# Hybrid attention block on one core: probabilities times values as two fp32r passes over four heads at once

## The chip, the cores and the metric

The kernel runs on one core of one Trainium2 chip, as one launch. The metric is the device time of an execution in microseconds (us), the median of repeated runs. TensorE is called PE (its weight loads PEld), VectorE DVE, ScalarE ACT, GpSimd POOL, SyncE SP. "fp32r" is the type in which PE takes a 32-bit operand in one pass at reduced precision; a full-precision operand is carried as a pair of fp32r tiles, "high" (the rounded value) and "low" (what the rounding left).

## What is computed

A transformer block on 512 tokens of width 1024: a mixer with three attention branches (a: stick-breaking, b: attention over the keys that an index score selects, c: a gated sum of compressed, selected-block and windowed attention), then attention over a memory of 256 tokens, then a gated feed-forward layer. Only branches b and c matter here. For each of them, cut to the core:

```python
s = jnp.einsum('bqhd,bkd->bhqk', qb, k) * scale      # four heads share one key head
p = _masked_softmax(s, mask)
o = jnp.einsum('bhqk,bkd->bqhd', p.astype(v.dtype), v)   # four heads share one value head, 64 wide
# branch c: gb[...,0:1]*o_cmp + gb[...,1:2]*o_sel + gb[...,2:3]*o_win
```

With 512 tokens, every selected block and the window cover all earlier keys, so `o_sel` and `o_win` are causal attention over two different key and value sets; branch b takes the 128 best keys of each query by its score. `o_cmp` runs over at most 31 compressed keys.

## The kernel before, in words

The kernel is written for a scheduler that takes the program order as priority: it lays out each engine's queue when the program is built, moving an instruction ahead of others that are not ready. So matrix products of later parts fill PE while the attention chains wait on other engines. Buffers come from pools; a tile name in a pool is a ring of `bufs` buffers.

Weights come through two rings. `load_split` (line 88) takes a raw buffer (name "raw", three of them in the pool `stage`), lets SP load 512 KB into it, copies the high part on ACT (line 58) and subtracts the low part on DVE (line 66) into one of three buffer pairs ("whi", "wlo"). `load_fill` (line 89) is the same with two buffers of each kind in the pool `fill`, and its subtraction runs on POOL. A product of two split operands is `mm3` (lines 91 to 96): high by high, high by low, low by high, all fp32r.

The part around the change, in program order: the projections (lines 524 to 552); the loop of branch c over four row tiles of 128 queries (lines 619 to 624); the gates of branch a (`fill_gate(0, f)`, line 627) and its up-projection (`merge_up(0, ...)`, 628); the gates of branch c (630); the 16 rounds that pick the top 128 scores, on DVE (631 to 633); the up-projection of branch c (634, weights through `load_split`); the masks from the scores (638); the loop of branch b over four row tiles (640 to 643); the gates of branch b (646), eight products named f = 0 to 7 over half the tokens, of which the odd ones take their weights through `load_split` and the even ones through `load_fill` (line 378); then the memory's norm, keys and values (663 to 683, weights through `load_split`).

A row tile of attention is `rows_attention` (570 to 590): per head two products give the scores (line 292, 293), DVE adds the mask and finds the negated maximum (578), ACT takes the exponential and its sum (579); then the rows are scaled (586 on ACT in branch c, 588 on DVE in branch b), and `apply_v` (561 to 568) runs once for each 128 keys: four transposes on PE into one PSUM bank (565), one copy to SBUF (568 calls line 58 on ACT for branch c, line 60 on DVE for branch b), and `pair` (98 to 101): two full fp32 products of the 64-wide value with two heads' probabilities each (256 columns), one into PSUM partitions 0 to 63 and one into 64 to 127. `cmp_attention` (592 to 610) does the same for the compressed keys with 32-row transposes. A row tile ends with `split(..., scale=0.5)` from PSUM into o_hi (68, ACT) and o_lo (69, DVE).

The constants (identity, masks, rotary tables) are one tile `cst`, loaded in two pieces (191, 305).

Of the kernel before, what the change touches and what calls it, by code (L numbers as in the profile page):

```python
# [26 lines left out]
def block_kernel(ctx: ExitStack, tc: tile.TileContext, A, out, dbg=None):  # L27
# [13 lines left out]
    fill_st = ctx.enter_context(ExitStack())  # L41
    fill = pool(fill_st, "fill", side="right")
    utp = pool(ctx, "ut")
    cst = const.tile([P, 1408], F32, name="cst")
    nc.scalar.preload_act_table_set("natural_log_exp_and_others")
    ident = cst[:, 0:128]
    causal = cst[:, 384:896]
    cmpb = cst[:, 896:1024].rearrange("p (h n) -> p h n", n=32)
    rope_t = cst[:, 1024:1536 - 128].rearrange("p (t c d) -> p t c d", t=3, d=32)
    eps = const.tile([P, 1], F32, name="eps")  # L50
    nc.vector.memset(eps, 1e-6)
    one = const.tile([P, 1], F32, name="one")
# [93 lines left out]
    def cc(c):  # L146
        return slice(c * P, (c + 1) * P)
# [154 lines left out]
    for c in range(NT):  # L302
        for i, post in enumerate((post_qa, post_ka, post_va)):
            project_chunk(c, 256, w_a[8 * i:8 * i + 8], post)
    nc.sync.dma_start(cst[:, 128:], A["cst"][:, 128:])
    nc.vector.memset(fixed[:, 3, :].bitcast(F32), -1.0)
    nc.vector.tensor_copy(fixed[:, 0:3, :], cst[:, 0:384].rearrange("p (a b) -> p a b", b=128))
    flush()
    w0_st.close()

# [115 lines left out]
    kwin = k_pair(bc, "kwin")  # L426
    vs = {n: bc.tile([P, NT, 64], F32, name=n) for n in ("vb", "vsel", "vwin")}
    kc = k_pair(bc, "kc", 32)
    vc = bc.tile([32, 64], F32, name="vc")
    score = [None] + [bc.tile([P, (i + 1) * P], F32, name=f"score{i}") for i in range(1, NT)]  # L430
    early_st = mix.enter_context(ExitStack())
    early = pool(early_st, "early")
# [5 lines left out]
    cw = pool(cw_st, "cw")  # L438
    pw_st = mix.enter_context(ExitStack())
    pw = pool(pw_st, "pw2")  # L440

    def post_g1(c, p):

# [54 lines left out]
    def compressed(hid):  # L498
        hs = cw.tile([P, 512], F32, name="rel", bufs=2)
        v, t = hs[0:32, 0:256], hs[0:32, 256:512]  # L500
        nc.scalar.copy(v, hid[0:32].rearrange("p a b -> p (a b)"))
        nc.vector.tensor_mul(t, v, v)
        nc.vector.tensor_scalar(t, t, 0.044715, 1.0, op0=ALU.mult, op1=ALU.add)
        nc.vector.tensor_mul(t, t, v)
        nc.scalar.activation(t, t, AF.Exp, scale=-1.5957691216057308)
        nc.vector.tensor_scalar(t, t, 1.0, None, op0=ALU.add)
        nc.vector.reciprocal(t, t)
        nc.vector.tensor_mul(v, v, t)
        tp = ps.tile([P, 512], F32, name="ps")
        for x in range(2):  # L510
            nc.tensor.transpose(tp[:, 32 * x:32 * x + 32], v[:, 128 * x:128 * x + 128], ident[0:32, 0:32])
        ht = cw.tile([P, 2, 32], F32, name="ht")
        nc.vector.tensor_copy(ht, tp[:, 0:64].rearrange("p (a b) -> p a b", b=32))
        w2t = cw.tile([P, 3, 64], F32, name="w2t")
        for i in range(2):
            nc.scalar.dma_start(w2t[:, i, :], A["cmp_w2_k"][0])
        nc.scalar.dma_start(w2t[:, 2, :], A["cmp_w2_v"][0])
        res = ps.tile([P, 512], F32, name="ps")
        nc.tensor.matmul(res[:, 0:32], w2t[:, 0:2, :].rearrange("p a d -> p (a d)"), ht[:, 0, :], start=True, stop=True)
        nc.tensor.matmul(res[0:32, 64:128], ht[:, 1, :], w2t[:, 2, :], start=True, stop=True)  # L520
        split(kc[0], kc[1], res[:, 0:32])
        nc.vector.tensor_copy(vc, res[0:32, 64:128])

    project([(1732, 256)], 4, post_g2)
    project([(1024, 128), (1408, 68), (1988, 140)], 3, post_g1)
# [32 lines left out]
    mq_st = mix.enter_context(ExitStack())  # L558
    mq = pool(mq_st, "mq")

    def apply_v(o_ps, v, src, first, last, k=P, eng=nc.scalar):

        tp = ps.tile([P, 4, P], F32, name="ps")
        for h in range(4):
            nc.tensor.transpose(tp[0:k, h, :], src[:, h, :], ident)
        pt = mq.tile([P, 4, P], F32, name="pt", bufs=3)
        copy(eng, pt[0:k], tp[0:k])
        pair(o_ps, [v, v], [pt[0:k, x::2, :] for x in range(2)], first, last)

    def rows_attention(i, q, k, v, bias, gate, o_ps, first, last, eng=nc.scalar):  # L570
        n = (i + 1) * P
        pr = mq.tile([P, 4, 512], F32, name="pr", bufs=2)
        nm = mq.tile([P, 4], F32, name="nm", bufs=2)
        den = mq.tile([P, 4], F32, name="den", bufs=2)
        for h in range(4):
            st = gm_ps.tile([P, 512], F32, name="gm")
            scores(st[:, :n], q[:, h, cc(i)], [t[:, 0:n] for t in k])
            nc.vector.tensor_tensor_reduce(pr[:, h, :n], st[:, :n], bias, -1.0, 3e38, ALU.add, ALU.min, nm[:, h:h + 1])
            nc.scalar.activation(pr[:, h, :n], pr[:, h, :n], AF.Exp, bias=nm[:, h:h + 1], scale=-1.0, accum_out=den[:, h:h + 1])
        sc = mq.tile([P, 4], F32, name="sc", bufs=2)  # L580
        nc.vector.reciprocal(sc, den)
        if gate is not None:
            nc.vector.tensor_mul(sc, sc, gate)
        for h in range(4):
            if eng is nc.scalar:
                nc.scalar.activation(pr[:, h, :n], pr[:, h, :n], AF.Copy, scale=sc[:, h:h + 1])
            else:
                nc.vector.tensor_scalar(pr[:, h, :n], pr[:, h, :n], sc[:, h:h + 1], None, op0=ALU.mult)
        for j in range(i + 1):
            apply_v(o_ps, v[:, j, :], pr[:, :, cc(j)], first and j == 0, last and j == i, eng=eng)  # L590

    def cmp_attention(i, o_ps, first, last):
        s = mq.tile([P, 4, 32], F32, name="cs")
        st = ps.tile([P, 4, P], F32, name="ps")
        for h in range(4):
            scores(st[:, h, 0:32], qc[:, h, cc(i)], kc)
        nc.vector.tensor_add(s, st[:, :, 0:32], cmpb[:, i, :].unsqueeze(1).to_broadcast([P, 4, 32]))
        m = mq.tile([P, 4], F32, name="nm", bufs=2)
        nc.vector.tensor_reduce(m, s, axis=AX.X, op=ALU.max)
        nc.vector.tensor_scalar(m, m, -1e20, None, op0=ALU.max)  # L600
        nc.vector.tensor_sub(s, s, m.unsqueeze(2).to_broadcast([P, 4, 32]))
        nc.scalar.activation(s, s, AF.Exp)
        den = mq.tile([P, 4], F32, name="den", bufs=2)
        nc.vector.tensor_reduce(den, s, axis=AX.X, op=ALU.add)
        nc.vector.tensor_scalar(den, den, 1e-30, None, op0=ALU.max)
        sc = mq.tile([P, 4], F32, name="sc", bufs=2)
        nc.vector.reciprocal(sc, den)
        nc.vector.tensor_mul(sc, sc, gates[:, i, 0::3])
        nc.vector.tensor_mul(s, s, sc.unsqueeze(2).to_broadcast([P, 4, 32]))
        apply_v(o_ps, vc, s, first, last, k=32)  # L610

    def topk_rounds(i, n):
        for _ in range(n):
            m8 = mq.tile([P, 8], F32, name="m8", bufs=3)
            nc.vector.max(m8, score[i])
            nc.vector.match_replace(score[i], m8, score[i], -3e38)

    o_c = o_pair("c", mq)
    for i in range(NT):
        o_ps = av_ps.tile([P, 2, P], F32, name="av")  # L620
        cmp_attention(i, o_ps, True, False)
        rows_attention(i, qc, ksel, vs["vsel"], causal_bias(i), gates[:, i, 1::3], o_ps, False, False)
        rows_attention(i, qc, kwin, vs["vwin"], causal_bias(i), gates[:, i, 2::3], o_ps, False, True)
        split(o_c[0][:, :, cc(i)], o_c[1][:, :, cc(i)], o_ps, scale=0.5)
    dump("o_c", o_c[0].bitcast(F32))
    for f in range(early_g, NK):
        fill_gate(0, f)
# [9 lines left out]
    for i in range(1, NT):  # L637
        nc.vector.tensor_scalar(score[i], score[i], -2e38, NEG, op0=ALU.is_gt, op1=ALU.mult)
    o_b = o_pair("b", op)
    for i in range(NT):  # L640
        o_ps = av_ps.tile([P, 2, P], F32, name="av")
        rows_attention(i, qb, kb, vs["vb"], score[i] if i else causal_bias(0), None, o_ps, True, True, nc.vector)
        split(o_b[0][:, :, cc(i)], o_b[1][:, :, cc(i)], o_ps, scale=0.5)
    dump("o_b", o_b[0].bitcast(F32))
    for f in range(NK):
        fill_gate(1, f, S // 2)
# [234 lines left out]
def constants():  # L881
    import numpy as np

    c = np.zeros((128, 1408), np.float32)
    i = np.arange(128)
    c[:, 0:128] = np.eye(128, dtype=np.float32)
    c[:, 128:256] = np.where(i[:, None] >= i[None, :], -1.0, 0.0)
    c[:, 256:384] = np.where(i[:, None] >= i[None, :], NEG, 0.0)
    c[:, 768:896] = np.where(i[None, :] > i[:, None], NEG, 0.0)
    n = np.arange(32)  # L890
    for t in range(4):
        q = t * 128 + i
        c[:, 896 + 32 * t:928 + 32 * t] = np.where((16 * n[None, :] + 31 <= q[:, None]) & (n[None, :] < 31), 0.0, NEG)
    inv = np.float32(10000.0) ** (-np.arange(0, 64, 2, dtype=np.float32) / np.float32(64))
    ang = np.arange(512, dtype=np.float32)[:, None] * inv[None, :].astype(np.float32)
    cos, sin = np.cos(ang), np.sin(ang)
    for t, tab in enumerate((cos, -sin, sin)):
        c[:, 1024 + 128 * t:1152 + 128 * t] = tab.reshape(4, 128, 32).transpose(1, 0, 2).reshape(128, 128)
    return c
# [26 lines left out]
```

## Time and profile before

| | us |
|---|---|
| median of 3 runs (lowest, highest) | 902.41 (901.3, 902.61) |
| the profiled execution's own time | 901.59 |
| its span, first to last instruction | 899.8 |
| PE busy in the span | 859.8 (96%) |
| DVE, ACT, POOL busy | 509.5, 412.3, 139.0 |
| mean granted TensorE clock | 0.990 |

Times in rows are from the span's start. A busy share of PE counts the pipeline of each matmul, so overlapping matmuls are counted once; how fast PE works is read from the distance between matmuls, not from the busy share. In the chain view each piece is the time that one step adds to the chain that ended last. "x4" is a count of instructions; one fp32 product is recorded as two instructions.

### The profile page before, as it was taken

What the parts mean: (1) busy time and instruction counts of PE and PEld (TensorE: products, weight loads), DVE (VectorE), ACT (ScalarE), POOL (GpSimd) and SP (SyncE); (2) the same over time, 40 slices, a digit from 0 to 9 for tenths busy, and PEclk for the clock granted to TensorE, in tenths of its full rate; (3) what the DMA queues carried; (4) which work ended last, traced back from release to release, by engine and by line L of the source; (5) the groups of instructions that cost most, each with busy time, mean ns of one, the idle gap of its engine ahead of it and who ended that gap; (6) DMA issues with size and microseconds to landing.
All of it is one profiled execution on the core that took longest, in us unless ns stands there. A gap on an engine that the chain in (4) does not pass through costs nothing.

```text
span 899.8 us, 13079 instructions
## 1 busy us (share of the span) xinstructions
PE 859.8 (96%) x5012; PEld 734.3 (82%) x5012; DVE 509.5 (57%) x1155; ACT 412.3 (46%) x779; POOL 139.0 (15%) x116
## 2 busy tenths in 40 slices
PE   5999999899999999899989999999999999999995
PEld 5987899887768877778878979998888888888884
DVE  4456378799992067676677758544434333322226
ACT  6488545567772234554655546432232233211123
POOL 4021232202224462230232020000000000000002
PEclk9999999999999999999999999999999999999998
DMA  9340114511212332558445514553333333332312
GB/s 322 84 110 24 52 49 121 139 48 34 62 48 71 94 94 71 186 173 241 128 148 187 178 48 131 179 160 93 94 95 101 105 98 94 117 94 93 97 45 93
DMA packets 93710, 99.00 MB, mean 110 GB/s; under 512 B 4656, under 2 KB 81616, under 8 KB 93648
## 3 DMA queue, kind: packets, MB, share of 16 engines
q1 hardware_dynamic: 91568, 92.75, 34.1%
q10 hardware_dynamic: 2080, 5.42, 1.8%
q8 instruction: 39, 0.64, 0.3%
q14 instruction: 23, 0.19, 0.1%
HBM read 96.06 MB, written 2.10 MB: 109 GB/s over the span
## 4 chain that ended last, share of the span: by engine, by line
PE 83%; DVE 8%; ACT 3%; DMA 3%; issue 2%; POOL 1%; SPq 0%; ACTq 0%; DVEq 0%; POOLq 0%
PE wo L95 9%; PE wo L96 9%; PE wo L94 9%; PE gf L94 5%; PE gf L96 5%; PE gf L95 5%; PE ff L96 4%; PE ff L94 4%; PE ff L95 4%; PE gm L94 3%; PE gm L95 3%; PE gm L96 3%; PE av L101 2%; PE y L96 2%; PE y L95 2%; PE y L94 2%
## 5 line engine op out<-in xcount | busy, mean ns | idle before, releaser
L58 ACT CAST whi<-raw 128x1024 fp32r<-128x1024 f32 (+1 forms) x167 | 174.9, 1050 | 289.0 <-PE y L96 78.9
L66 DVE TENSOR_TENSOR wlo<-raw,whi 128x1024 fp32r<-128x1024 f32 (+1 forms) x131 | 164.2, 1256 | 206.6 <-ACT whi L58 206.2
L66 POOL TENSOR_TENSOR wlo<-raw,whi 128x1024 fp32r<-128x1024 f32 x36 | 87.2, 2428 | 324.2 <-ACT whi L58 277.2
L95 PE MATMUL wo<-ut_lo,whi 128*128 128x256 f32 (+1 forms) x320 | 105.9, 331 | 0.0
L96 PE MATMUL wo<-ut_hi,wlo 128*128 128x256 f32 (+1 forms) x320 | 105.0, 328 | 0.0
L94 PE MATMUL wo<-ut_hi,whi 128*128 128x256 f32 (+1 forms) x320 | 104.7, 327 | 0.0
L96 PE MATMUL gf<-ut_hi,wlo 128*128 128x512 f32 (+1 forms) x192 | 70.0, 365 | 0.0
L94 PE MATMUL gf<-ut_hi,whi 128*128 128x512 f32 (+1 forms) x192 | 69.8, 364 | 0.0
L95 PE MATMUL gf<-ut_lo,whi 128*128 128x512 f32 (+1 forms) x192 | 69.5, 362 | 0.0
L94 PE MATMUL ff<-ut_hi,whi 128*128 128x512 f32 (+1 forms) x192 | 67.9, 354 | 0.0
L95 PE MATMUL ff<-ut_lo,whi 128*128 128x512 f32 (+1 forms) x192 | 67.9, 354 | 0.0
L96 PE MATMUL ff<-ut_hi,wlo 128*128 128x512 f32 (+1 forms) x192 | 67.9, 354 | 0.0
L95 PEld LDWEIGHTS wo<-ut_lo,whi 128*128 128x128 f32 x320 | 61.4, 192 | 6.3 <-issue 1.0
L94 PEld LDWEIGHTS wo<-ut_hi,whi 128*128 128x128 f32 x320 | 61.2, 191 | 5.7 <-issue 0.7
L96 PEld LDWEIGHTS wo<-ut_hi,wlo 128*128 128x128 f32 x320 | 61.3, 192 | 5.5 <-issue 0.4
L875 POOL TENSOR_TENSOR ut_hi<-ut_hi,ut_lo 128x512 f32<-128x512 f32 x4 | 5.0, 1274 | 367.0 <-ACT ut_hi L874 367.0
L94 PE MATMUL gm<-whi,ut_hi 128*128 128x256 f32 (+1 forms) x160 | 47.6, 298 | 0.0
L95 PE MATMUL gm<-wlo,ut_hi 128*128 128x256 f32 (+1 forms) x160 | 46.7, 292 | 0.0
L96 PE MATMUL gm<-whi,ut_lo 128*128 128x256 f32 (+1 forms) x160 | 46.6, 291 | 0.0
L96 PEld LDWEIGHTS gf<-ut_hi,wlo 128*128 128x128 f32 x192 | 36.2, 189 | 6.6 <-issue 1.9
L94 PEld LDWEIGHTS gf<-ut_hi,whi 128*128 128x128 f32 x192 | 36.2, 189 | 6.3 <-issue 1.5
L95 PEld LDWEIGHTS gf<-ut_lo,whi 128*128 128x128 f32 x192 | 36.3, 189 | 5.5 <-issue 0.8
(329 smaller groups left out, 2034.8 us busy)
## 6 DMA issues: line engine op xcount, KB each, us to landing
raw<-in_w_ffn_in_dram SPq DMA_DIRECT2D x56, 512.0 KB, 3.6
raw<-in_w_in_dram SPq DMA_DIRECT2D x46, 512.0 KB, 3.9
raw<-in_w_ffn_out_dram SPq DMA_DIRECT2D x22, 512.0 KB, 3.6
raw<-in_w_out_dram SPq DMA_DIRECT2D x16, 512.0 KB, 3.6
raw<-in_w_up_dram SPq DMA_DIRECT2D x8, 512.0 KB, 3.8
xt<-in_x_dram SPq DMA_DIRECT2D x4, 512.0 KB, 9.2
raw<-in_w_mem_kv_dram SPq DMA_DIRECT2D x4, 512.0 KB, 3.7
raw<-in_w_mem_q_dram SPq DMA_DIRECT2D x4, 512.0 KB, 3.7
```

Source lines behind the costliest of these rows:

```text
L58: nc.scalar.copy(dst, src)
L66: (lo_eng or nc.vector).tensor_sub(dst_lo, src, dst_hi.bitcast(F32))
L94: nc.tensor.matmul(dst, lh, rh, start=first, stop=False, skip_group_check=True)
L95: nc.tensor.matmul(dst, lh, rl, start=False, stop=False, skip_group_check=True)
L96: return nc.tensor.matmul(dst, ll, rh, start=False, stop=last, skip_group_check=True).ins
L101: nc.tensor.matmul(dst[64 * x:64 * x + 64], lhs[x], rhs[x], start=first, stop=last, skip_group_check=True)
L875: nc.gpsimd.tensor_mul(yo[:, n], yo[:, n], gain[:, n])
```

## The change

`apply_v` makes both operands pairs of fp32r. The value of one key tile is stored as its high and low parts side by side in 128 columns; the probabilities of all four heads (512 columns) are the moving operand, once their high part and once their low part. The result fills a whole PSUM bank: partitions 0 to 63 hold what the high part of the value gives, 64 to 127 what its low part gives. After the last key tile of a row tile, the new function `fold` adds the two halves and puts heads where they stood before; its SBUF tile is a "raw" buffer of the pool `stage`. The compressed branch is padded with zeros to 128 keys and takes its rows from the ring "pr". The constants are re-ordered, and the rotary tables and two triangular masks are loaded into pools of their own.

```diff
-    cst = const.tile([P, 1408], F32, name="cst")
+    cst = const.tile([P, 768], F32, name="cst")
...
-    nc.sync.dma_start(cst[:, 128:], A["cst"][:, 128:])
+    tri = pw.tile([P, 2, 128], F32, name="tri")
+    nc.sync.dma_start(tri, A["cst"][:, 768:1024].rearrange("p (a b) -> p a b", b=128))
+    nc.sync.dma_start(cst[:, 128:], A["cst"][:, 128:768])
...
-    nc.vector.tensor_copy(fixed[:, 0:3, :], cst[:, 0:384].rearrange("p (a b) -> p a b", b=128))
+    nc.vector.tensor_copy(fixed[:, 0, :], ident)
+    nc.vector.tensor_copy(fixed[:, 1:3, :], tri)
...
-    vc = bc.tile([32, 64], F32, name="vc")
+    vc = bc.tile([P, 2, 64], F32R, name="vc")
+    nc.gpsimd.memset(vc.bitcast(F32), 0.0)
...
+    rope_t = pw.tile([P, 3, NT, 32], F32, name="rope_t")
+    nc.sync.dma_start(rope_t, A["cst"][:, 1024:1408].rearrange("p (t c d) -> p t c d", t=3, d=32))
...
-        nc.vector.tensor_copy(vc, res[0:32, 64:128])
+        split(vc[0:32, 0, :], vc[0:32, 1, :], res[0:32, 64:128])
...
-    def apply_v(o_ps, v, src, first, last, k=P, eng=nc.scalar):
+    def apply_v(o_ps, v, src, first, last):
         tp = ps.tile([P, 4, P], F32, name="ps")
         for h in range(4):
-            nc.tensor.transpose(tp[0:k, h, :], src[:, h, :], ident)
-        pt = mq.tile([P, 4, P], F32, name="pt", bufs=3)
-        copy(eng, pt[0:k], tp[0:k])
-        pair(o_ps, [v, v], [pt[0:k, x::2, :] for x in range(2)], first, last)
+            nc.tensor.transpose(tp[:, h, :], src[:, h, :], ident)
+        pt = [mq.tile([P, 4, P], F32R, name=n, bufs=2) for n in ("pt_hi", "pt_lo")]
+        split(pt[0], pt[1], tp)
+        for x in range(2):
+            nc.tensor.matmul(o_ps, v.rearrange("p a d -> p (a d)"), pt[x].rearrange("p h q -> p (h q)"),
+                             start=first and x == 0, stop=last and x == 1, skip_group_check=True)
+
+    def fold(o, i, o_ps):
+        ov = o_ps.rearrange("p (a b q) -> p a b q", a=2, b=2)
+        hi, lo = (t[:, :, cc(i)] for t in o)
+        t = stage.tile([P, WT], F32, name="raw", bufs=3)[:, 0:2 * P].rearrange("p (a q) -> p a q", a=2)
+        top, bot = slice(0, 64), slice(64, 128)
+        nc.scalar.copy(t[top], ov[bot, :, 0, :])
+        nc.scalar.copy(t[bot], ov[top, :, 1, :])
+        nc.vector.tensor_add(t[top], ov[top, :, 0, :], t[top])
+        nc.vector.tensor_add(t[bot], ov[bot, :, 1, :], t[bot])
+        split(hi, lo, t, scale=0.5)
...
-        s = mq.tile([P, 4, 32], F32, name="cs")
+        pr = mq.tile([P, 4, 512], F32, name="pr", bufs=2)
+        s = pr[:, :, 0:32]
+        nc.gpsimd.memset(pr[:, :, 32:128], 0.0)
...
-        apply_v(o_ps, vc, s, first, last, k=32)
+        apply_v(o_ps, vc, pr[:, :, 0:128], first, last)
...
+    def two_parts(v):
+        t = mq.tile([P, NT, 2, 64], F32R, name="v2", bufs=2)
+        split(t[:, :, 0, :], t[:, :, 1, :], v)
+        return t
+
+    vsel, vwin = two_parts(vs["vsel"]), two_parts(vs["vwin"])
...
-        o_ps = av_ps.tile([P, 2, P], F32, name="av")
+        o_ps = av_ps.tile([P, 512], F32, name="av")
...
-        split(o_c[0][:, :, cc(i)], o_c[1][:, :, cc(i)], o_ps, scale=0.5)
+        fold(o_c, i, o_ps)
...
+    vb = two_parts(vs["vb"])
...
-        split(o_b[0][:, :, cc(i)], o_b[1][:, :, cc(i)], o_ps, scale=0.5)
+        fold(o_b, i, o_ps)
```

## Rows read from the trace of the kernel before

**Rows 1.** The page, busy time by engine.
```profile
PE 859.8 (96%) x5012; PEld 734.3 (82%) x5012; DVE 509.5 (57%) x1155; ACT 412.3 (46%) x779; POOL 139.0 (15%) x116
```

**Rows 2.** Busy time by stretch: window, length, engines, PE clock, DMA share, GB/s.
```profile
195.00:329.00 134.00, 133.01 (x689) 101.33 (x688) 83.54 (x283) 71.27 (x159) 44.42 (x21) 1.00 0.25 67
329.00:360.00 31.00, 29.30 (x206) 22.79 (x205) 24.74 (x69) 16.12 (x43) 8.42 (x5) 1.00 0.23 69
372.00:377.00 5.00, 0.73 (x8) 0.52 (x6) 4.89 (x5) 2.06 (x4) 3.32 (x2) 0.99 0.75 258
377.00:381.00 4.00, 4.00 (x15) 3.06 (x16) 2.78 (x4) 2.11 (x6) 0.00 (x0) 0.58 0.45 115
```

**Rows 3.** The chain that ended last, 345 to 400 us: start, length, step.
```profile
358.60 0.58 PE av L101 x4
...
376.99 1.09 PE ps L133 x4
...
390.47 0.23 PE gm L96
```

**Rows 4.** Groups of PE's matmuls by shape, 359.2 to 372 us.
```profile
L94 PE MATMUL gf<-ut_hi,whi 128*128 128x256 f32 x35 | 10.0, 285 | 0.0
```

**Rows 5.** Line 101, its instructions: count, ns min/median/max, first and last start.
```profile
L101 PE MATMUL av<-pt,vb x40: 379/404/430, 336.1 to 358.8; 128*64 128x256 f32 x40
```

**Rows 6.** The chain that ended last, 196 to 270 us.
```profile
204.06 0.58 PE av L101 x4
204.65 0.43 PE gf L95
...
234.48 1.45 PE av L101 x12
```

**Rows 7.** Instructions in order of time, 256 to 264 us: PE's matmuls and weight loads.
```profile
259.30 0.40 PE L96 MATMUL gf<-o_hi,wlo 128*128 128x512 f32 x1
259.30 0.19 PEld L94 LDWEIGHTS gf<-o_hi,whi 128*128 128x128 f32 x1
...
259.53 0.40 PE L94 MATMUL gf<-o_hi,whi 128*128 128x512 f32 x1
```

**Rows 8.** Groups of DVE by shape, 329 to 361 us: busy us, mean ns.
```profile
L60 DVE COPY pt<-ps 128x512 f32<-128x512 f32 x10 | 6.4, 687 | 2.4 <-PE ps L565 2.2
...
L66 DVE TENSOR_TENSOR wlo<-raw,whi 128x1024 fp32r<-128x1024 f32 x2 | 2.6, 1304 | 0.0
...
L69 DVE SCALAR_TENSOR_TENSOR o_lo<-av,o_hi 128x256 fp32r<-128x256 f32 x4 | 1.7, 424 | 2.3 <-ACT o_hi L68 2.3
```

**Rows 9.** The instructions on tile pt: the copy on ACT.
```profile
L58 ACT COPY pt<-ps x24: 560/590/617, 201.0 to 267.2; 128x512 f32<-128x512 f32 x20, 32x512 f32<-32x512 f32 x4
```

**Rows 10.** Groups of ACT by shape, 329 to 361 us.
```profile
L58 ACT CAST whi<-raw 128x1024 fp32r<-128x1024 f32 x4 | 4.2, 1048 | 7.0 <-PE gm L95 5.4 <-PE gf L95 1.2 <-issue 0.4
...
L68 ACT ACTIVATE o_hi<-av 128x256 fp32r<-128x256 f32 x4 | 1.5, 384 | 7.8 <-PE av L101 7.8
```

**Rows 11.** Line 616, the last step of the top-128 rounds.
```profile
L616 DVE MATCH_REPLACE8 score<-m,score x48: 409/550/708, 196.6 to 271.8; 128x256 f32<-128x256 f32 x16, 128x384 f32<-128x384 f32 x16, 128x512 f32<-128x512 f32 x16
```

**Rows 12.** The page, DMA issues: KB each, median us to landing.
```profile
raw<-in_w_in_dram SPq DMA_DIRECT2D x46, 512.0 KB, 3.9
```

**Rows 13.** Instructions of DVE in order of time, 63 to 67.2 us.
```profile
65.43 1.16 DVE L66 TENSOR_TENSOR sbwl<-sbs,sbwh 128x512 fp32r<-128x512 f32 x2 [3.45 <-ACT sbwh L58]
66.69 0.69 DVE L331 SCALAR_TENSOR_TENSOR sbs<-ps,sba 128x512 f32<-128x512 f32 x1
```

**Rows 14.** Instructions of ACT in order of time, 62 to 67 us.
```profile
62.29 0.72 ACT L329 ACTIVATE sba<-sba,one 128x512 f32<-128x512 f32 x1
...
66.34 0.30 ACT L345 ACTIVATE sbs<-ps 128x128 f32<-128x128 f32 x1
```

**Rows 15.** The instructions on tile wlo, DVE alone, 180 to 330 us.
```profile
L66 DVE TENSOR_TENSOR wlo<-raw,whi x3: 1204/1206/1847, 190.2 to 323.6; 128x1024 fp32r<-128x1024 f32 x3
```

**Rows 16.** Instructions of SP in order of time, 190 to 209 us.
```profile
191.38 17.05 SPq L80 DMA_DIRECT2D raw<-in_w_in_dram  x3
```

More of the change, by code (lines that the diff above doesn't have):

```diff
@@ L43, in block_kernel @@
     utp = pool(ctx, "ut")
-    cst = const.tile([P, 1408], F32, name="cst")
+    cst = const.tile([P, 768], F32, name="cst")
     nc.scalar.preload_act_table_set("natural_log_exp_and_others")
     ident = cst[:, 0:128]
-    causal = cst[:, 384:896]
-    cmpb = cst[:, 896:1024].rearrange("p (h n) -> p h n", n=32)
-    rope_t = cst[:, 1024:1536 - 128].rearrange("p (t c d) -> p t c d", t=3, d=32)
+    causal = cst[:, 128:640]
+    cmpb = cst[:, 640:768].rearrange("p (h n) -> p h n", n=32)
     eps = const.tile([P, 1], F32, name="eps")
@@ L589, in rows_attention @@
         for j in range(i + 1):
-            apply_v(o_ps, v[:, j, :], pr[:, :, cc(j)], first and j == 0, last and j == i, eng=eng)
+            apply_v(o_ps, v[:, j, :, :], pr[:, :, cc(j)], first and j == 0, last and j == i)
     def cmp_attention(i, o_ps, first, last):
-        s = mq.tile([P, 4, 32], F32, name="cs")
+        pr = mq.tile([P, 4, 512], F32, name="pr", bufs=2)
+        s = pr[:, :, 0:32]
+        nc.gpsimd.memset(pr[:, :, 32:128], 0.0)
         st = ps.tile([P, 4, P], F32, name="ps")
@@ L616, in topk_rounds @@
             nc.vector.match_replace(score[i], m8, score[i], -3e38)
+    def two_parts(v):
[3 more added lines that the diff above has]
+    vsel, vwin = two_parts(vs["vsel"]), two_parts(vs["vwin"])
     o_c = o_pair("c", mq)
     for i in range(NT):
-        o_ps = av_ps.tile([P, 2, P], F32, name="av")
+        o_ps = av_ps.tile([P, 512], F32, name="av")
         cmp_attention(i, o_ps, True, False)
-        rows_attention(i, qc, ksel, vs["vsel"], causal_bias(i), gates[:, i, 1::3], o_ps, False, False)
-        rows_attention(i, qc, kwin, vs["vwin"], causal_bias(i), gates[:, i, 2::3], o_ps, False, True)
-        split(o_c[0][:, :, cc(i)], o_c[1][:, :, cc(i)], o_ps, scale=0.5)
+        rows_attention(i, qc, ksel, vsel, causal_bias(i), gates[:, i, 1::3], o_ps, False, False)
+        rows_attention(i, qc, kwin, vwin, causal_bias(i), gates[:, i, 2::3], o_ps, False, True)
+        fold(o_c, i, o_ps)
     dump("o_c", o_c[0].bitcast(F32))
@@ L639, in block_kernel @@
     o_b = o_pair("b", op)
+    vb = two_parts(vs["vb"])
     for i in range(NT):
-        o_ps = av_ps.tile([P, 2, P], F32, name="av")
-        rows_attention(i, qb, kb, vs["vb"], score[i] if i else causal_bias(0), None, o_ps, True, True, nc.vector)
-        split(o_b[0][:, :, cc(i)], o_b[1][:, :, cc(i)], o_ps, scale=0.5)
+        o_ps = av_ps.tile([P, 512], F32, name="av")
+        rows_attention(i, qb, kb, vb, score[i] if i else causal_bias(0), None, o_ps, True, True, nc.vector)
+        fold(o_b, i, o_ps)
     dump("o_b", o_b[0].bitcast(F32))
@@ L886, in constants @@
     c[:, 0:128] = np.eye(128, dtype=np.float32)
-    c[:, 128:256] = np.where(i[:, None] >= i[None, :], -1.0, 0.0)
-    c[:, 256:384] = np.where(i[:, None] >= i[None, :], NEG, 0.0)
-    c[:, 768:896] = np.where(i[None, :] > i[:, None], NEG, 0.0)
+    c[:, 768:896] = np.where(i[:, None] >= i[None, :], -1.0, 0.0)
+    c[:, 896:1024] = np.where(i[:, None] >= i[None, :], NEG, 0.0)
+    c[:, 512:640] = np.where(i[None, :] > i[:, None], NEG, 0.0)
     n = np.arange(32)
@@ L892, in constants @@
         q = t * 128 + i
-        c[:, 896 + 32 * t:928 + 32 * t] = np.where((16 * n[None, :] + 31 <= q[:, None]) & (n[None, :] < 31), 0.0, NEG)
+        c[:, 640 + 32 * t:672 + 32 * t] = np.where((16 * n[None, :] + 31 <= q[:, None]) & (n[None, :] < 31), 0.0, NEG)
     inv = np.float32(10000.0) ** (-np.arange(0, 64, 2, dtype=np.float32) / np.float32(64))
```

## The prediction

> **What bounds the kernel now.** I read the page first: PE is busy for 859.8 of 899.8 us [rows 1], so the first question is whether PE is the limit where the change acts. The stretch view answers it in two halves. From 195 to 329 us (branch c, gates, up-projections) PE is busy 133.01 of 134 us and DVE 83.54 [rows 2]; gate products fill every hole, so what PE saves there moves the end. From 329 to 360 us (branch b) PE is busy 29.30 and DVE 24.74 of 31 us [rows 2]: neither is full, and the chain through both sets the pace. Of PE's 206 matmuls there, 32 are scores, 40 transposes and 40 products with values [rows 5], so 94, nearly four gates of 24, are filler. After branch b's last product at 358.60 + 0.58 = 359.2 us, 105 gate matmuls (3 lines of 35) are left and run until 372 [rows 4]. Then PE is nearly idle for 5 us and restarts at a granted clock of 0.58, mostly the lower level of 1.2 GHz [rows 2], because the memory's norm, which starts when branch b ends, delivers only at 376.99; its keys and values end at 390.7 [rows 3]. So 31.5 us lie between branch b's last product and that point.
>
> **PE's products.** One key tile is four recorded instructions on line 101. The chain gives 0.58 us for a lone one and 1.45 for three in a row, so each further one costs (1.45 - 0.58) / 2 = 0.435. The gate matmul that follows takes 0.43 [rows 6] instead of the 0.23 between neighbours [rows 7]: leaving costs 0.20. I counted 15 runs over branch c's 24 key tiles (9 single, 3 double, 3 triple), so 15 x 0.78 + 9 x 0.435 = 15.6 us; branch b has 10 single ones, 7.8 us. After: two fp32r matmuls of 512 columns. The nearest rows are the gate's, 0.23 apart, with the next weights loading in 0.19 us inside the matmul before [rows 7]; I take 0.47 a tile: 24 x 0.47 = 11.3 and 10 x 0.47 = 4.7. Saved: 4.3 in branch c plus what stalls around short runs give, say **4.7 us** (bounds 3.5 and 6), all on the path because PE is full; and 3.1 us in branch b, in part on the path.
> A rule speaks against this: the Trainium skill, TensorE: Matmul & The Clock Gate (Part 3, The mechanism), says that a weight load overlaps running matmuls only when its row group differs. Both passes use all rows, so by it each pass would show its load; rows 7 show the opposite for equal shapes. It is the third rival below.
>
> **What DVE and ACT get.** In branch c the copy stays on ACT (0.59 us [rows 9]) and a DVE subtraction is new: nearest row the DVE copy from PSUM of the same size, 0.69 [rows 8], so 24 x 0.69 = 16.6 us. The folds add two DVE additions of half a tile, at 0.42 as for o_lo [rows 8], and two ACT copies at 0.38 as for o_hi [rows 10]: 3.4 and 3.1 us in each branch. Making value pairs costs 0.4 on each engine three times; splitting the compressed value less. On DVE that is some 21 us beside the 83.54 of 134 [rows 2]. They push back the top-128 rounds, last in priority, from 271.8 [rows 11] to about 293; branch b needs them at 324, so 30 us of slack hide it. If that cover were gone, PE would wait. The compressed rows now share ring "pr" and need a POOL memset, and the accumulator is released after the additions: both lengthen branch c's chain, hidden by 45 us of gate c products behind it. The transposes keep their count; I cost them at nothing. The constants: the masks come earlier in smaller loads, a gain or loss under 0.5 us under the first weights; the rotary tables load after the first branch frees memory, and one 3.9-us load [rows 12] lands about when they are first read; a miss would delay one chunk's post-processing under the projections' products. Zero for these, bounds -0.5 and +1.
>
> **The hidden move: whose turn is a raw buffer.** `fold` takes a "raw" buffer of the ring that feeds `load_split`. The trace shows that one ring's buffers are taken in program order: in the stick-breaking branch a head's first "sbs" input is ready at 62.29 + 0.72 = 63.0 [rows 14], DVE then idles 3.45 us, and the write comes at 66.69 [rows 13], only after the previous head's last "sbs" was taken at 66.34 [rows 14]. Now the program order of "raw" is: branch c's four folds, its up-projection weights, branch b's four folds, the odd gates of branch b (f = 1, 3, 5, 7), the memory's key and value weights. Before, odd gates were loaded at 191.38 us and just after, ahead of branch c [rows 16], and waited raw until buffers came free: line 66 ran three times on DVE from 180 to 330 us, first at 190.2, last at 323.6 [rows 15]. Now their turn comes only with the last fold of branch b. Gates also take PSUM banks in order, so f = 1 holds up 2 to 7. Branch b keeps 24 filler matmuls instead of 94. The up-projection of branch c also loads later, at about 285 instead of before 195; it is needed at 312, so nothing.
>
> **The sum.** Branch b starts 4.7 us earlier, at 324.3. How long is it to the last product, 30.2 us before? Below: DVE's own work, 24.7 less two weight subtractions (2.6 [rows 8]) and the last o_lo (0.4), plus three folds' additions (2.5) makes 24.2. Above: 30.2 less 3.1 of PE, plus one ACT hop of 0.6 in each of four row tiles, plus 2.5 of additions, 32.0. Less filler also means less waiting behind it. I take 29.5, nearer the upper end since DVE was 80% busy before: last product at 353.8, that is 5.4 early. Then f = 1: two fold copies (0.8), the high cast (1.05 [rows 10]) and the subtraction (1.3 [rows 8]) make 3.2 if the load has landed; with a load of 3.9 us first, 7. I take 5.5, PE idle. Then 168 gate matmuls (12 us for 105 [rows 4], so 19.3), the memory's transposes (16 at 0.11) and 48 products at 0.23 (together 12.8), now without the second idle. About 1.7 for the lower clock after an idle stretch, as at 377 to 381, is paid as before. Sum from the last product 39.3, against 31.5: +7.8. Net -5.4 + 7.8 = **+2.4 us**. Later parts only shift. The profiled execution took 901.59, so 904.0; the median of the runs shown is 0.8 higher, so I predict 904.8, slower by 0.27%. A measurement of this kernel can tell about 0.2%, 1.8 us, from no change.
>
> **Rivals.** (1) Filler is not starved: the odd gates get buffers before the last fold. For it: nothing in the arithmetic needs the fold's buffer to be "raw", and three buffers exist. Against: rows 13 and 14. Then 4.7 is kept, and of branch b's 3.1 some 1.5: 902.4 - 6 = 896.4, faster. Chance 0.20.
> (2) Starved, but branch b runs so much freer that it cancels: with a chain of 27.5 instead of 29.5 us the sum is +0.4, 902.8. For it: DVE's 24.2 leave room. Against: each product now waits for two engines in turn. Chance 0.28 for the same time, and 0.05 for a gain from the same cause.
> (3) Weights show: each fp32r pass of the change pays its load of 0.19 [rows 7] in branch c, 48 x 0.19 = 9.1 us, so 913.9. It decides if 512-column passes run over 0.40 apart. Chance 0.03, since the gates' rows refute it.
> (4) My forecast, slower through the starved gap. Chance 0.44.
> Slower has 0.47, no change 0.28, faster 0.25. The range reaches from rival 1 to a starved gap of 7 us with a branch b of 32 and a lowered clock in it (+2.4 + 2.5 + 1.5 + 1, 909.8): 896 to 910.
>
> **What would show it.** Right: line 101's place taken by pairs of matmuls 0.23 apart; PE full to about 324 us; branch b with about 24 gate matmuls and DVE the busier engine; the odd gates' loads or at least their ACT casts only after the last fold; PE idle for 3 to 7 us right after branch b, and no second idle before the memory's products. Wrong: gate matmuls still interleaved with branch b in their old number; PE stalls before 324 on the new subtraction; top-128 rounds ending after 320.

## The result, and the profile after

The kernel after takes 909.5 us (median of 4 runs, 907.6 to 910.41), the kernel before beside it 901.97 (901.3 to 902.61): ratio 1.0069, 95% interval [1.0052, 1.0086]. The ratio is worked out from all runs together; 0.69% is 6.2 us, the two medians are 7.5 us apart. It is slower, as forecast, and inside the forecast range, but by 6 to 7.5 us instead of 2.4. The profiled execution took 909.58 us with a span of 907.8, 8.0 more than before. The page's busy line answers to [rows 1]:

```profile
PE 860.6 (95%) x4944; PEld 739.5 (81%) x4944; DVE 530.1 (58%) x1199; ACT 423.2 (47%) x809; POOL 139.9 (15%) x121
```

PE has 68 recorded instructions less (34 key tiles, two instead of four each), DVE 20.6 us more work. The busy times by stretch of the kernel after (columns as in [rows 2]), cut at branch b's first score (329.7), its last product (359.5) and the gates behind it:

```profile
195.00:329.70 134.70, 132.64 (x644) 105.68 (x643) 104.78 (x320) 76.06 (x172) 45.78 (x24) 1.00 0.24 67
329.70:359.50 29.80, 23.40 (x117) 16.25 (x115) 25.29 (x72) 19.40 (x53) 4.95 (x4) 0.94 0.29 89
359.50:363.60 4.10, 0.00 (x0) 0.00 (x0) 2.06 (x8) 3.15 (x7) 0.00 (x0) 0.71 0.43 139
363.60:386.00 22.40, 22.32 (x169) 22.03 (x170) 11.26 (x20) 11.02 (x17) 6.51 (x3) 0.90 0.71 205
386.00:400.00 14.00, 13.30 (x65) 10.42 (x63) 7.50 (x9) 9.51 (x18) 0.68 (x1) 1.00 0.49 158
```

Two things are seen. First, the stretch of branch c is no shorter: branch b starts at 329.7 where it started at 329.0, although DVE does 104.8 us there instead of some 84, and PE has 45 recorded instructions less there (644 against 689 [rows 2]). Second, PE has nothing at all for 4.1 us after branch b, and then 168 gate products take 22.4 us at a granted clock of 0.90. The chain that ended last shows why (columns as in [rows 3]):

```profile
358.97 0.52 PE av L574
359.51 0.34 ACT raw L583
359.89 0.37 ACT raw L584
360.29 0.42 DVE raw L585
360.72 0.44 DVE raw L586
361.18 0.42 ACT o_hi L67
...
363.83 1.24 DVE wlo L65
365.11 0.58 PE gf L95
...
399.78 0.23 PE gm L95
```

The fold (lines 583 to 587) runs right behind the last product. Only then come the casts of the odd gates' weights. Instructions of the kernel after in order of time: SP's loads into the ring from 300 to 366 us, then from 358.5 to 366.2 us the fold's first copy, the last subtraction that reads the fold's buffer, a load into that buffer, and the high cast and the low subtraction of the first odd gate:

```profile
347.93 17.52 SPq L79 DMA_DIRECT2D raw<-in_w_in_dram  x4
...
359.51 0.37 ACT L583 COPY raw<-av 64x256 f32<-64x256 f32 x1 [1.32 <-PE av L574]
...
361.63 0.42 DVE L68 SCALAR_TENSOR_TENSOR o_lo<-raw,o_hi 128x256 fp32r<-128x256 f32 x1 [0.48 <-ACT o_hi L67]
362.08 3.37 SPq L79 DMA_DIRECT2D raw<-in_w_in_dram  x2
...
362.54 1.03 ACT L57 CAST whi<-raw 128x1024 fp32r<-128x1024 f32 x1
...
363.83 1.23 DVE L65 TENSOR_TENSOR wlo<-raw,whi 128x1024 fp32r<-128x1024 f32 x1
```

The load at 362.08 is not that of the first odd gate. With three buffers, each of the first three odd gates takes the buffer of an earlier fold: the loads go out at 347.93, 355.16 and 362.08, each within 0.04 us of the end of the subtraction that reads the second, third and fourth fold's buffer. The first one has landed at 351.70. Its cast still runs at 362.54, behind the last fold's copies in ACT's queue, although ACT stood idle for 1.32 us before them. So in the end it was the place of the cast in ACT's queue, laid out when the program was built, and not the buffer itself, that held the first gate; why the scheduler put it there is not shown.

The memory's keys and values end at 400.0 instead of 390.7 [rows 3]: 9.3 us late, of which 0.7 was there when branch b began, -0.4 came in it and 9.0 behind it. Later parts give 1.3 back.

### The profile page after: what moved, and what is told of

Its sections match the earlier page's. It is cut to its first block, busy times and chain, and to the rows that moved or that the text cites. A ratio compares the mean times of both kernels' runs of the same rounds, so it can differ in the third digit from the quotient of the medians.

```text
span 907.8 us, 13051 instructions
## 1 busy us (share of the span) xinstructions
PE 860.6 (95%) x4944; PEld 739.5 (81%) x4944; DVE 530.1 (58%) x1199; ACT 423.2 (47%) x809; POOL 139.9 (15%) x121
## 4 chain that ended last, share of the span: by engine, by line
PE 80%; DVE 10%; ACT 4%; issue 2%; DMA 2%; POOL 0%; ACTq 0%; DVEq 0%; POOLq 0%
PE wo L94 8%; PE wo L95 8%; PE wo L93 8%; PE gf L94 5%; PE gf L95 5%; PE gf L93 5%; PE ff L95 4%; PE ff L94 4%; PE ff L93 4%; PE gm L93 2%; PE gm L94 2%; PE gm L95 2%; PE y L94 2%; PE y L95 2%; PE y L93 2%
```

## Where branch c's saving went

The new products are as cheap as forecast. Passes over the values on line 574, the place of line 101, in both branches (columns as in [rows 5], then idle time before passes and weight loads together: us, times):

```profile
L574 PE MATMUL av<-pt_hi,v x30: 392/400/510, 204.8 to 358.2; 128*128 128x512 f32 x30
...
L574 PE MATMUL av<-pt_lo,v x30: 388/397/742, 205.8 to 359.0; 128*128 128x512 f32 x30
...
  ACT pt_hi L57: 8.0, 17
  DVE pt_lo L65: 4.4, 12
```

To see what PE's work would take without waiting, I summed the distances between the ends of neighbouring products, from branch c's first compressed score to branch b's first score, and counted as waiting what a distance has over the usual one of its two kinds of neighbours. Before: 132.5 us of work and 1.2 of waiting. After: 128.9 and 5.6. So some 3 to 3.6 us of work were saved and some 4 us of waiting came in their place (such a split depends by 1 to 2 us on what is taken as usual: with the median of each pair of kinds, and a key tile's old products counted as one, it is 130.9 and 2.7 before, 128.0 and 6.6 after). The waits view, 195 to 332 us, which takes in the first 2 to 3 us of branch b, says for whom (us in total, times, longest; up to branch b's first score the first lines are 0.9 before and 4.5 after). Before:

```profile
PEld gm L292 <- DVE nm L578: 1.4, 4, 0.6
...
PE gm L292 <- DVE nm L578: 0.6, 2, 0.4
```

After:

```profile
PEld gm L291 <- DVE nm L597: 4.7, 9, 1.4
...
PE gm L291 <- DVE nm L597: 1.8, 3, 1.0
```

Scores wait for a PSUM bank that DVE's mask step has not yet read. A score that waits also holds the gate products queued behind it. One such wait, in order of time:

```profile
226.94 0.40 PE L574 MATMUL av<-pt_lo,v 128*128 128x512 f32 x1
226.94 0.19 PEld L574 LDWEIGHTS av<-pt_hi,v 128*128 128x128 f32 x1
227.15 2.38 POOL L65 TENSOR_TENSOR wlo<-raw,whi 128x1024 fp32r<-128x1024 f32 x1 [7.20 <-ACT whi L57]
227.17 0.39 PE L574 MATMUL av<-pt_hi,v 128*128 128x512 f32 x1
...
227.39 0.55 DVE L597 CUSTOM_DVE_ANT_0 pr<-gm,cst 128x384 f32<-128x384 f32 x1
...
227.86 1.70 DVE L621 TENSOR_SCALAR nm<-nm 128x4 f32<-128x4 f32 x1
...
229.47 0.54 DVE L597 CUSTOM_DVE_ANT_0 pr<-gm,cst 128x384 f32<-128x384 f32 x1
...
230.08 0.45 PE L291 MATMUL gm<-ksel_hi,qc 128*128 128x384 f32 x1 [1.00 <-DVE nm L597]
...
230.54 0.39 PE L94 MATMUL gf<-ut_lo,whi 128*128 128x512 f32 x1
```

The passes run 0.23 us apart with the next weights (0.19) inside the pass before. The next mask stands behind a four-column operation that takes 1.70 us; the same line takes 0.17 in the other three row tiles. It ends when POOL's weight subtraction ends (227.15 + 2.38 = 229.53, against 229.56). So there are two candidates for the lateness of DVE: too much work on it, and single operations held beside POOL.

## The experiments

All twelve in one table. "b at" is branch b's first score, "b" the time to its last product, "inside" the gate products of branch b that are issued ahead of that last product (all within branch b but one at most; in e12 17 of the 130 come before it begins), "to kv" the time from branch b's start to the end of the memory's keys and values (profiled execution); the ratio is to the kernel before on the same chip. The profiled executions of e1, e11 and e12 are the slowest of their runs, 1.8 to 2.2 us over the median. The scheduler lays out the queues anew for each kernel, so a difference between two of them holds a change of order too.

| kernel | ratio, 95% interval | b at | b | inside | to kv |
|---|---|---|---|---|---|
| before | 1 | 329.0 | 30.2 | 87 | 61.7 |
| after | 1.0069 [1.0052, 1.0086] | 329.7 | 29.8 | 24 | 70.3 |
| e1_own_buffer | 1.0112 [1.0098, 1.0126] | 336.7 | 34.2 | 111 | 64.4 |
| e2_before_raw_b | 1.0037 [1.0024, 1.005] | 331.0 | 24.2 | 24 | 66.0 |
| e3_before_raw_c | 1.0009 [1.0, 1.0018] | 329.3 | 30.2 | 87 | 62.4 |
| e4_no_low | 1.0058 [1.0046, 1.007] | 332.1 | 29.8 | 76 | 64.1 |
| e5_cmp_own | 1.0114 [1.0099, 1.0129] | 331.8 | 29.4 | 24 | 70.8 |
| e6_cmp_own_buffer | 1.0128 [1.0107, 1.015] | 336.6 | 34.2 | 111 | 62.5 |
| e7_c_only | 1.0114 [1.0101, 1.0127] | 338.2 | 29.7 | 83 | 63.3 |
| e8_b_only | 1.0034 [1.0021, 1.0046] | 330.5 | 34.2 | 111 | 64.1 |
| e9_own_no_topk | 1.0026 [1.0017, 1.0036] | 328.7 | 34.2 | 111 | 64.2 |
| e10_before_no_topk | 1.0003 [0.9992, 1.0014] | 329.3 | 30.2 | 87 | 62.6 |
| e11_own_topk_late | 1.0039 [1.0025, 1.0053] | 331.1 | 34.2 | 111 | 65.2 |
| e12_late_subs_dve | 1.0038 [1.0024, 1.0052] | 330.8 | 34.5 | 130 | 65.7 |

### The fold without the ring (e1_own_buffer)

The kernel after, with the fold's tile laid over value tiles that are no longer needed:

```diff
-        t = stage.tile([P, WT], F32, name="raw", bufs=3)[:, 0:2 * P].rearrange("p (a q) -> p a q", a=2)
+        t = vs[("vsel", "vwin")[i % 2]].rearrange("p (a c) d -> p a (c d)", a=2)
```

> The changed kernel with fold's tile laid over a value tile that is no longer read, not taken from the ring raw. Theory A (the turn in the ring raw starves branch b of gate products): about 94 gate products lie among branch b's again, no gap of 4 to 5 us before the first odd gate, and most of the loss goes, 901 to 903 us. Rival B (the longer chain of a key tile, copy then subtraction, and the fold make the loss; the ring does nothing): unchanged, 908 to 910 us, with gates still behind branch b.

The filler came back (111 gate products) and "to kv" fell by 5.9 us, yet the whole got slower, 910.84 us, because branch b started 7.0 us later. The waits view of this kernel, from 195 us to branch b's start:

```profile
PEld gm L291 <- DVE nm L597: 4.9, 7, 2.3
...
PE ps L570 <- ACT pr L605: 1.6, 1, 1.6
```

By the same split as above, PE's work is 128.3 us, as in the kernel after, and the waiting 11.8. So the buffer explains the part behind branch b, and a second cost, in branch c, is larger when the queue is laid out this way. Not all of these 11.8 us are waits. The longest wait, and the busy times of the stretch around it:

```profile
258.09 2.33 DVE L622 TENSOR_TENSOR pr<-pr,nm 128x128 f32<-128x128 f32 x1
...
261.09 0.50 PE L291 MATMUL gm<-ksel_hi,qc 128*128 128x512 f32 x1 [1.89 <-DVE nm L597]
```

```profile
255.00:265.00 10.00, 7.54 (x26) 5.13 (x25) 9.53 (x26) 5.35 (x13) 2.35 (x1) 0.84 0.20 52
```

The DVE operation ran beside a POOL subtraction (2.35 us from 257.92), and PE's wait of 1.6 us in the view above follows another such one (2.35 us from 274.96). Behind the first wait the granted clock fell: 0.84 of 10 us loses 1.6 us on top of the pause. Branch c of e6, e7 and e11 has such a fall too (0.66 from 205 to 210, from 205 to 215 and from 230 to 235 us); up to branch b the kernels before and after, e4, e5, e8, e9 and e10 have none.

### The touch alone (e2_before_raw_b and e3_before_raw_c)

The kernel before, with one column copied into a "raw" buffer after each row tile, in branch b (e2) or in branch c (e3):

```diff
+        nc.scalar.copy(stage.tile([P, WT], F32, name="raw", bufs=3)[:, 0:1], o_ps[:, 0, 0:1])
```

> The kernel before, where each row tile of branch b also copies one column of its result into a buffer of the ring raw (0.2 us of ACT each); products, copies and folds as before. Theory A: the odd gates wait for branch b's end, 168 gate products behind it instead of 105, and the time is 907 to 911 us. Rival B: 902 to 903 us.

> The same touch in branch c alone. Theory A: the up-projection weights of branch c and the odd gates load after branch c (from about 270 us), long before their use at 317, so the time stays at 901.5 to 903 us. A rival by which any later load of these weights costs: over 905 us.

One column is enough. Busy times by stretch of e2, columns as above:

```profile
331.00:355.20 24.20, 21.10 (x137) 13.72 (x135) 20.32 (x66) 12.14 (x40) 4.97 (x4) 1.00 0.22 66
355.20:357.50 2.30, 0.02 (x3) 0.01 (x1) 0.45 (x2) 1.55 (x4) 0.00 (x0) 1.00 0.50 153
357.50:383.10 25.60, 23.65 (x170) 23.15 (x171) 13.98 (x24) 11.87 (x19) 7.42 (x3) 0.87 0.71 231
```

Branch b is 6.0 us shorter for want of filler, PE is idle for 2.3 us, and 168 gate products follow at a clock of 0.87: "to kv" grows by 4.3 us, the time by 0.37%. The same touch in branch c costs 0.09%, at the edge of what can be told. The hidden move is shown, and it needs neither the fold's arithmetic nor the new products. Its price in the kernel before was put too high: 904.78 us, where 907 to 911 was expected.

### One pass's low part left out (e4_no_low)

e1 with both passes taking the high part of the probabilities; the low part's share of the result and its 34 subtractions are left out:

```diff
...
-        split(pt[0], pt[1], tp)
+        nc.scalar.copy(pt[0], tp)
...
-            nc.tensor.matmul(o_ps, v.rearrange("p a d -> p (a d)"), pt[x].rearrange("p h q -> p (h q)"),
+            nc.tensor.matmul(o_ps, v.rearrange("p a d -> p (a d)"), pt[0].rearrange("p h q -> p (h q)"),
```

> As e1, without the subtraction that makes the probabilities' low part: both passes take the high part (the low part's share of the result is left out, the high one counted twice). PE's work is that of e1, DVE has 34 x 0.69 us less. Theory C (branch c's saving on PE was given back because PE, in order, waited for DVE, which the subtractions crowd): branch b starts 4 to 5 us before 329 and the time is 4 to 6 us under e1's. Rival D (the two passes are no cheaper on PE than the four fp32 ones): branch b starts at 329 again and the time is within 2 us of e1's.

Against e1 the waiting in branch c fell from 11.8 to 7.2 us, branch b began 4.6 us earlier, and the ratio fell from 1.0112 to 1.0058. The new subtractions matter, but without them branch b still begins 3.1 us later than before, where 4 to 5 us earlier was expected.

### The compressed rows apart (e5_cmp_own, e6_cmp_own_buffer)

The kernel after (e5) and e1 (e6), with the compressed branch's rows 32 wide in a tile of their own again: no buffer of the ring "pr", no memset, and passes over 32 rows. (In e6 and e7 the fold's tile is the same value tile for every row tile.)

```diff
-        pr = mq.tile([P, 4, 512], F32, name="pr", bufs=2)
-        s = pr[:, :, 0:32]
-        nc.gpsimd.memset(pr[:, :, 32:128], 0.0)
+        s = vs["vwin"][:, :, 0:32]
...
-        apply_v(o_ps, vc, pr[:, :, 0:128], first, last)
+        apply_v(o_ps, vc, s, first, last, k=32)
```

> The changed kernel, but the compressed rows stay 32 wide in a tile of their own (a value tile no longer read) instead of a zero-padded buffer of the ring pr; transposes and passes over 32 rows. Theory E (the third user of the two pr buffers holds the next row tile's scores in their banks, and PE waits in order): PE's waits on line 597 in branch c fall from 6.5 us to under 2, branch b starts 3 to 5 us earlier than 329.7, and the time is 904 to 907 us. Rival (those waits come from DVE being crowded by the subtractions): unchanged, 908 to 911 us.

> As e5, and fold's tile not from the ring raw. Theory E plus the ring's turn (3 us by the touch in branch b): branch b starts by 326 and has its gate products again; 902 to 905 us. If branch b's own chain (copy, then subtraction, before each product) is the larger part, branch b still lasts 33 to 35 us with its filler and the time is 905 to 908 us.

Neither moved branch b's start to an earlier time (331.8 against 329.7, 336.6 against 336.7). So no gain was seen from giving up the shared ring. In e6 the profiled execution, 908.33 us, lies well below the median of 912.47, so its columns show the order of things and not the time.

### One branch at a time (e7_c_only, e8_b_only)

e7 has the new products in branch c alone (as e6; branch b's fp32 probabilities in two buffers instead of three), e8 in branch b alone (the fold as in e1; branch c's fp32 probabilities in two buffers instead of three). The choice, in `rows_attention` of e7; e8 has the two calls exchanged:

```diff
+            if eng is nc.scalar:
+                apply_v(o_ps, v[:, j, :, :], pr[:, :, cc(j)], first and j == 0, last and j == i)
+            else:
+                apply_old(o_ps, v[:, j, :], pr[:, :, cc(j)], first and j == 0, last and j == i, eng)
```

> The new products in branch c alone, with the compressed rows and fold's tile as in e6; branch b has its old fp32 products and DVE copies. If branch c's passes are worth 4.7 us on PE and nothing else holds it: 896.5 to 899 us. If PE's in-order waits eat it: 901 to 903 us, with branch b starting at 328 to 330.

> The new products in branch b alone, fold's tile not from the ring raw; branch c as before (its fp32 probabilities in two buffers instead of three). If the extra hop from ACT to DVE lengthens branch b's chain with filler beside it: branch b lasts 33 to 35 us instead of 30.2 and the time is 904 to 907 us. If the saved 3.1 us of PE count: 899 to 901 us.

Branch c alone costs 1.14% (910.96 us, where 903 at most was expected), and branch b, without the ring, 0.34%. In e7 some 3.4 us of the loss are the lowered clock from 205 to 215 us (0.66 of 10 us), behind a wait of 1.6 us. In e8 branch b starts 1.5 us later than before and is 4.0 us longer, but takes in 24 more gate products: "to kv" is 2.4 us longer. Up to 1.6 us of that is a lower clock between 375 and 385 us (0.78 and 0.54 in its halves, before 0.69 and 0.96). So the new products cost a little in branch b too, in this build, and the larger loss sits in branch c.

### Less on DVE (e9_own_no_topk, e10_before_no_topk)

e1 and the kernel before, each with 1 instead of 16 selection rounds; 15 rounds are left out of both.

```diff
-    for r in range(16):
+    for r in range(1):
```

> The own-buffer kernel (fold does not use the raw ring) with 1 instead of 16 top-128 rounds; what is left out is 15 of the 16 selection rounds, so branch b's mask is not the reference's. Compared with the before kernel treated the same way. Theory C (crowded DVE): TensorE's in-order waits in branch c, which ate the 4.7 us that the new products save, come from DVE being late with masks, subtractions and folds because the selection rounds and the new subtractions share it. With some 40 us of DVE work gone from that stretch, it falls from 140.1 us (own buffer) to 131 or less, and the time falls by 6 us or more against the own-buffer kernel, to about 904. Rival D (the two hops of the new products, copy then subtraction, and the order in which TensorE's queue was laid out, whatever else DVE has to do): the stretch stays at 136 or more.

> The control: the kernel before with 1 instead of 16 top-128 rounds (15 selection rounds left out). Its TensorE was full in that stretch, so both theories expect little: stretch 133.7 us +- 1, time within 2 us of the kernel before. If it falls by 3 us or more, the selection rounds cost TensorE time in the kernel before too, and what they cost in the changed kernel is less special.

Busy times by stretch, first e9, then e10:

```profile
195.20:328.70 133.50, 131.00 (x637) 104.22 (x636) 62.92 (x183) 75.79 (x170) 45.74 (x24) 1.00 0.24 67
```

```profile
195.20:329.30 134.10, 132.69 (x685) 100.93 (x684) 39.84 (x147) 70.76 (x159) 44.22 (x21) 1.00 0.25 67
```

With DVE at 63 instead of 107 us, branch b of e9 starts 8.0 us earlier than in e1, and the ratio falls from 1.0112 to 1.0026. The control does not move (1.0003). So the same selection rounds that cost the kernel before nothing cost e1 0.86%, some 7.7 us, the fall of its clock among them: crowding is shown as the main cause of e1's loss in branch c. For the kernel after, whose branch b starts 7.0 us earlier than e1's, the rounds were not priced. Nor is crowding the whole: the stretch is 133.5 us, not the 131 or less that was expected. Work is 128.5 us there, waiting still 5.1.

### The rounds later, nothing left out (e11_own_topk_late)

e1 with every selection round queued on DVE behind branch c's last fold:

```diff
...
-        for x in range(1, NT):
-            topk_rounds(x, 1)
+        with tc.issue_after(last_c):
+            for x in range(1, NT):
+                topk_rounds(x, 1)
```

> The own-buffer kernel with all 16 selection rounds queued on DVE behind branch c's last fold, nothing left out. Theory C: DVE is free for branch c while it runs, so the stretch falls to about 131 to 133 us; the rounds (some 45 us) end at about 315, still ahead of branch b; with branch b at 34 us and 62 to 64 us from its start to the memory's keys and values, the time is about 900 to 903, as the kernel before or faster. Rival D: the stretch stays at 137 or more and the time at 908 or more. If the rounds end after branch c's up-projection, branch b waits for its masks and the stretch is longer than 140.

The result lies between the two: 906.45 us, branch b at 331.1, 5.6 us earlier than in e1. Busy times by stretch, then one wait in order of time:

```profile
195.00:271.00 76.00, 74.12 (x388) 59.40 (x387) 48.95 (x158) 59.58 (x149) 15.63 (x9) 0.98 0.16 46
271.00:321.00 50.00, 49.97 (x214) 39.74 (x212) 49.20 (x149) 14.54 (x20) 20.86 (x9) 1.00 0.33 90
```

```profile
226.76 2.39 POOL L65 TENSOR_TENSOR wlo<-raw,whi 128x1024 fp32r<-128x1024 f32 x1 [2.92 <-ACT whi L57]
...
227.14 2.29 DVE L588 SCALAR_TENSOR_TENSOR o_lo<-vwin,o_hi 128x256 fp32r<-128x256 f32 x1
...
230.03 0.44 PE L291 MATMUL gm<-kwin_hi,qc 128*128 128x384 f32 x1 [1.44 <-DVE nm L598]
```

Branch c now ends at 270.9 instead of 286.0. DVE is then full for 50 us with the rounds, and PE full beside it. The longest thing left in branch c is one held operation, 2.29 us where the free ones take 0.42, behind it 1.8 us without a new product, and then the fall of the clock (0.98 of 76 us loses 1.5 us).

### The held operations (e12_late_subs_dve)

e11 with the seven weight subtractions that fall into branch c on DVE instead of POOL:

```diff
...
+    load_pool, load_fill = load_fill, ring(fill, (2, 2), lo_eng=nc.vector)
     for f in range(early_g, NK):
         fill_gate(0, f)
     merge_up(0, "a", load_fill, gf_ps)
+    load_fill = load_pool
```

> The kernel with late selection rounds, and the low halves of the seven weight loads that fall into branch c (gates of branch a from f = 3 and its up-projection) subtracted on DVE instead of POOL, nothing left out. Theory H (held operations): in branch c the longest TensorE waits follow small SBUF-to-SBUF operations of DVE that take 1.1 to 2.4 us instead of 0.16 to 0.42 while POOL runs a 2.4-us weight subtraction (o_lo, 2.29 us at 227.14 in the kernel with late rounds, then 1.88 us without a TensorE product). With no POOL subtraction beside branch c no such operation is left there between 200 and 260 us, TensorE's waits fall from 7.9 to about 5 us, the stretch from 136.1 to 133 or 134 and the time from 906.5 to 903 or 904. Rival W (plain lateness): the long operations are not due to POOL, or the seven subtractions of 1.23 us that DVE now runs itself, 8.6 us, delay the masks by as much; the stretch stays at 136 or more and the time at 906 or more.

The same o_lo in order of time, and further on the end of the selection rounds:

```profile
227.70 0.42 DVE L588 SCALAR_TENSOR_TENSOR o_lo<-vwin,o_hi 128x256 fp32r<-128x256 f32 x1
...
228.12 1.20 DVE L65 TENSOR_TENSOR wlo<-raw,whi 128x1024 fp32r<-128x1024 f32 x1
...
319.95 1.28 DVE L390 SCALAR_TENSOR_TENSOR g<-g,gm 128x512 f32<-128x512 f32 x2
320.69 0.50 PE L93 MATMUL gm<-o_hi,whi 128*128 128x512 f32 x1 [2.06 <-DVE g L390]
```

```profile
318.60:321.20 2.60, 0.54 (x3) 0.47 (x3) 2.57 (x8) 0.00 (x0) 0.48 (x1) 1.00 0.68 195
321.20:325.00 3.80, 3.80 (x11) 2.98 (x11) 3.23 (x5) 0.03 (x1) 2.58 (x3) 0.57 0.00 0
```

Without POOL beside it the operation takes 0.42 us, and the wait behind it is gone: the mechanism is shown. The gain is not: the ratio is 1.0038 against 1.0039. Branch c takes 75.2 us to its last product instead of 75.9, but the merge that frees a PSUM bank stands behind the last selection rounds, PE waits 2.06 us for it, and the clock granted after this pause is 0.57 for 3.8 us, near the lower level of 1.2 GHz. What DVE's seven subtractions cost in this kernel was not told apart. The wait has moved to another place: the first theory holds for the held operation, the second for the time. No version here beats the kernel before.

## Why the prediction was right, and where it was not

- **The hidden move** held in its outcome: 24 gate products inside branch b, 168 after it, the first odd gate's cast only after the last fold, PE idle for 4.1 us (forecast 5.5, range 3 to 7). One step was told wrong: the first two odd gates' buffers came with the second and third fold, not the last, and the first one's load had landed by 351.7. What came last was its cast, behind the last fold in ACT's queue. That is the forecast's case of 3.2 us, with two additions, o_hi and a step of the memory's norm ahead of the cast. From branch b's last product to the memory's keys and values it took 40.5 us, forecast 39.3. e1 and e2 show the cause. Rival 1 falls, and rival 2 with it: branch b lasted 29.8 us (forecast 29.5). Of the 94 filler products counted before, 86 lie inside branch b; seven come behind its last product and one is the up-projection's. The 63 that moved (168 less 105) do not depend on it.
- **The sign was in part luck.** Slower had a chance of 0.47, the range reached to both sides, and 909.5 us is close to its upper end. e1 gives the gate products back, which is the condition of rival 1, priced at 896.4 us; it took 910.84. So the change without the hidden move, as e1 built it, was slower too.
- **What PE saves in branch c** was somewhat less than forecast, 3 to 3.6 us against 4.7 (bounds 3.5 to 6). The step that failed is "all on the path because PE is full". It put branch b at 324.3; it came at 329.7, and these 5.4 us are nearly all of the 5.6 by which the sum missed the span's +8.0 (the rest, 0.3 in branch b, 1.2 behind it and -1.3 later, cancels but for 0.2). A full PE told that it did not wait before; it did not tell how little DVE could be delayed before it would. New subtractions and folds made DVE late, and gate products stood behind the waiting scores: e1 without the subtractions (e4) or without the rounds (e9) begins branch b 4.6 and 8.0 us earlier. Operations held beside POOL stand before the longest waits of the kernel after and of e1.
- **"30 us of slack hide it"** was right for the rounds themselves (last one at 293.1, forecast 293) and for the amount (DVE +20.7 us, forecast 21), but wrong as a verdict on DVE. The rounds are last in priority, yet e9 against e1 prices them at 7.7 us beside the new work (in e1's order of the queues), and e10 at nothing beside the old. What was named under "Wrong", PE stalls before 324, is what happened, though more on the masks than on the subtraction itself.
- **The shared ring "pr"**, costed at nothing, was no loss (e5, e6).
- **Rival 3**: passes are 0.23 us apart with their weights inside. The sentence quoted there from the Trainium skill, taken alone, does not hold for these shapes; the same section also lets a load run ahead when it goes to a background weight buffer, which would fit.

## What to carry to other kernels

A full engine with an in-order queue gives back what its chains lose: a product saved is time saved only if the engines that free its banks are not made later by the same change. Look at the DVE work between two masks, not only at DVE's share of the stretch: e11 left no DVE work out, moved the rounds, and began branch b 5.6 us earlier than e1. Before a scratch tile is taken from a pool, see whose turn it takes: one column copied into a weight ring in each row tile of branch b cost 0.37%. And a short pause of a full PE can cost more than its length, when the clock falls behind it (e1, e12).

## What the runs showed of the hardware

DVE operations on SBUF data that take 0.17 and 0.42 us took 1.70 and 2.29 us when they met a 2.4-us POOL subtraction (nm in the kernel after, o_lo in e11; 0.42 again in e12). They end 0.03 and 0.28 us after POOL's subtraction. The Trainium skill, SBUF — State Buffer (Who interferes with whom), says that a DVE instruction with two SBUF inputs, or one in a two-port mode, and a POOL instruction that reads SBUF exclude each other and that the later one blocks fully. The trace of e11 agrees, where o_lo has two such inputs; nm has one, and whether it ran in a two-port mode no trace shows. In the mask step (line 597), which reads PSUM and SBUF, no such length was seen.

After 2.6 us almost without products the granted clock in e12 was 0.57 for the next 3.8 us, and products of 512 columns came 0.43 us apart instead of 0.23. At 0.57 of the clock 3.8 us lose 3.8 x 0.43 = 1.6 us, on top of the pause.
